# An expert stage written as a pipeline over pairs of experts: w2 of a pair between the experts of the next, small products grouped, weights in whole blocks

## The chip, the cores and the metric

The kernel runs on one core of a Trainium2 chip. The metric is the device time of one execution in microseconds (us), the median of several runs. The engines are TensorE (PE), VectorE (DVE), ScalarE (ACT), GpSimd (POOL) and SyncE (SP), which here issues nearly all transfers. PE's weight loads have a row of their own, PEld.

## The reference

Two layers of a hybrid block (a delta rule, pooling and sparse attention) are followed by two layers of a second block. A layer of the second block is a mixing part, a layernorm, a mixture of experts and another layernorm. There are 256 tokens of 1024 channels, 16 experts in four groups, and each token goes to two experts of one group. An expert has w1 and w3, each 1024 x 512, and w2, 512 x 1024. The part that the change touches is this:

```python
for l in range(DEPTH):
    h = _mixing(x, w_in[l], ...)
    x = _layernorm(alpha * x + h, ln1_g[l], ln1_b[l])
    m = _hier_moe(x.reshape(bsz * seq, d), w_group[l], b_group[l], w_expert[l], b_expert[l],
                  w1[l], w3[l], w2[l]).reshape(bsz, seq, d)
    x = _layernorm(alpha * x + m, ln2_g[l], ln2_b[l])

def expert_block(args):
    xb, e = args
    h = jax.nn.silu(xb @ w1[e]) * (xb @ w3[e])
    return h @ w2[e]
```

The results of the two experts of a token are weighted by its gates and summed.

## The kernel before

All weights stream from HBM once. Everything is in float32 or in float32 split into a high and a low part, and a float32 product of 512 columns leaves two records in the trace.

The expert stage gives each expert 64 slots. A token that finds no slot is handled by `overflow`, a dense computation over all experts behind a branch on the largest count (L1679 and L1690), which these inputs do not enter. The stage goes through the experts in groups of four, and within a group in pairs:

- **Gathers.** A product of the tokens (two blocks of 128, high and low part, zsh and zsl) with a one-hot matrix D picks the tokens of the four experts' 256 slots, one chunk of 128 channels at a time: four products for each of eight chunks. ACT or DVE (`affine`, L481 and L487) turns a chunk into xg. The gather of chunk k + 1 stands between the products of chunks k and k + 1 of the group's first expert.
- **w1 and w3** of an expert: the 64 slots of xg are the stationary operand, so a product takes half of the array's columns. w1 goes to the first half (j = 0), w3 to the second (j = 1), by turns, over eight chunks. ACT copies the result to `a` (L1604).
- **silu** (L1541): four transposes of `a` on PE, then ACT and DVE make hTe, the transposed hidden values. That of a pair's first expert stands within the second expert's products (at k = SILU_K), together with the transposed one-hot gT and the slots' gates; that of the second behind them.
- **w2** of the pair: for each half hf of the 1024 output columns, the four f-chunks of the first expert on one half of the array's columns and then the four of the second on the other. ACT and DVE evict a half, times the gate, into a high and a low part, yh (L1622) and yl (L1623).
- **add**: four products a half (two blocks of tokens, yh and yl) bring the slots' results back to their tokens, into sums in PSUM (pacc). One half of the pair before is added behind each of the pair's experts.

The branch stands between expert 7 and expert 8. In the second layer `rows` (L1658 to L1668) follows it: it spreads the gain and the bias of the last layernorm over all partitions by 32 products with diagonal matrices. All products of the helper `mm` carry the line L341; groups are told apart by their operands.

The weights of a layer are 192 blocks of 128 x 2 x 512 (0.5 MB), in the order of use: 24 for each pair, eight for w1 and w3 of each expert and eight for w2. `stream` (L1385 to L1405) issues them on SP into slots that it takes in turn; a slot comes free when PE has used the block in it, and SP waits for that in its queue. Some slots hold half a block or a quarter, which makes two or four transfers of the block. Of a layer's blocks FIRST + len(SOON) = 41 are issued ahead of the stage, during the mixing; those in SOON go last of them. The products are written in the order above; the layer that records them moves some of them a few places.

## Time and profile before

| | |
|---|---|
| runs | 1613.25 us, median of 3 (1613.2 to 1615.9) |
| span of the profiled execution | 1613.4 us |
| PE, DVE, ACT, POOL busy | 1550.3, 823.6, 670.2, 106.0 us |
| expert stage of layer 0, first gather to last add | 864.47 to 1121.84 us |
| expert stage of layer 1, first gather to last add | 1335.83 to 1602.1 us |
| granted PE clock over the span | 0.9 and more in every fortieth |
| bytes moved | 344 MB, 214 GB/s on the mean |

The profile is one execution, 0.15 us over the median of the runs. Busy times are sums over the span; matmuls are pipelined, so the busy time of a group on PE counts records that overlap only once. Where a row shows idle time before an instruction, the name behind the arrow is what ended it. A window's clock of 1.00 is the upper level.

### The profile page before, as it was taken

To read this page: it belongs to the slowest core of one execution; us is meant where nothing else is said; L and a number is where in the kernel's file an instruction comes from. 1 tells how busy PE (TensorE), PEld (TensorE's weight loads), DVE (VectorE), ACT (ScalarE), POOL (GpSimd) and SP (SyncE) were. 2 spreads that over 40 slices of the span, in tenths; PEclk is the share of its full clock that TensorE was granted. 3 is DMA by queue.
4 is the path that set the end of the run, shared out by engine and by line. 5 is a ranking of instruction groups with operands and counts; after the bars stand their busy time and mean duration, and the time that the engine had idled before them with its cause. 6 is when DMAs were issued, how large, how long until landed. Compare 5 with 4: busy or idle time off the path is not lost. (4 is left out here: it accounts for less than half of the span.)

```text
span 1613.4 us, 25627 instructions
## 1 busy us (share of the span) xinstructions
PE 1550.3 (96%) x9825; PEld 1107.2 (69%) x9826; DVE 823.6 (51%) x1897; ACT 670.2 (42%) x1383; POOL 106.0 (7%) x102
## 2 busy tenths in 40 slices
PE   8899999998999999999999998998999999998996
PEld 7877999988779999877775343343877774444332
DVE  6778656768786567567554111113567544112112
ACT  6536545565365455465543111112665542111111
POOL 3410000114100000200001000001000001000000
PEclk9999999999999999999999999999999999999999
DMA  7412664555126645444678999992356687998970
GB/s 263 148 54 74 209 184 144 182 159 151 54 75 209 183 143 173 148 151 150 231 274 282 343 357 354 376 378 93 99 164 212 235 277 268 332 381 322 387 291 27
DMA packets 149331, 344.47 MB, mean 214 GB/s; under 512 B 12112, under 2 KB 16848, under 8 KB 149200
## 3 DMA queue, kind: packets, MB, share of 16 engines
q1 hardware_dynamic: 149200, 342.74, 63.6%
q8 instruction: 81, 1.33, 0.3%
q14 instruction: 50, 0.41, 0.1%
HBM read 341.64 MB, written 1.05 MB: 212 GB/s over the span
## 5 line engine op out<-in xcount | busy, mean ns | idle before, releaser
L376 DVE TENSOR_TENSOR lo<-w,hi 128x1024 fp32r<-128x1024 f32 (+3 forms) x235 | 289.0, 1230 | 156.9 <-ACT hi L375 154.9
L375 ACT CAST hi<-w 128x1024 fp32r<-128x1024 f32 (+2 forms) x258 | 268.0, 1040 | 226.7 <-PE pd L341 175.2
L341 PE MATMUL p<-w,xg 128*64 128x512 f32 (+1 forms) x1044 | 265.2, 596 | 1.5 <-ACT xg L487 0.8
L341 PE MATMUL pd<-hTh,hi 128*128 128x256 f32 x768 | 218.7, 285 | 0.0
L341 PE MATMUL pd<-hTl,hi 128*128 128x256 f32 x768 | 218.4, 284 | 0.0
L341 PE MATMUL pd<-hTh,lo 128*128 128x256 f32 x768 | 218.2, 284 | 0.0
L341 PEld LDWEIGHTS p<-w,xg 128*64 128x64 f32 x1044 | 75.0, 136 | 113.4 <-issue 93.2
L341 PE MATMUL p<-w,hTe 128*64 128x512 f32 x496 | 148.1, 599 | 0.0
L341 PEld LDWEIGHTS pd<-hTh,hi 128*128 128x128 f32 x768 | 147.2, 192 | 0.2
L341 PEld LDWEIGHTS pd<-hTl,hi 128*128 128x128 f32 x768 | 147.2, 192 | 0.1
L341 PEld LDWEIGHTS pd<-hTh,lo 128*128 128x128 f32 x768 | 147.2, 192 | 0.1
L1550 DVE SCALAR_TENSOR_TENSOR t<-t,p 128x256 f32<-128x256 f32 x32 | 13.5, 421 | 191.9 <-ACT t L1547 191.9
L341 PEld LDWEIGHTS p<-w,hTe 128*64 128x64 f32 x496 | 50.1, 136 | 79.5 <-issue 75.0
L341 PE MATMUL pd<-hi,xTh 128*128 128x512 f32 (+2 forms) x224 | 86.7, 387 | 0.0
L341 PE MATMUL pd<-hi,xTl 128*128 128x512 f32 (+2 forms) x224 | 85.8, 385 | 0.0
L341 PE MATMUL pd<-lo,xTh 128*128 128x512 f32 (+2 forms) x224 | 84.9, 379 | 0.0
L1623 DVE SCALAR_TENSOR_TENSOR yl<-p,gslot,yh 128x512 fp32r<-128x512 f32 x32 | 24.0, 750 | 112.6 <-ACT yh L1622 104.9
L1604 ACT COPY a<-p 128x512 f32<-128x512 f32 x32 | 18.8, 587 | 138.2 <-PE p L341 123.3
L1622 ACT ACTIVATE yh<-p,gslot 128x512 fp32r<-128x512 f32 x32 | 22.0, 687 | 126.9 <-PE p L341 116.9
L376 POOL TENSOR_TENSOR lo<-w,hi 128x1024 fp32r<-128x1024 f32 (+2 forms) x23 | 55.6, 2430 | 171.0 <-ACT hi L375 165.1
L341 PE MATMUL pd<-lo,hTh 128*128 128x512 f32 (+1 forms) x160 | 62.7, 392 | 0.5 <-POOL lo L376 0.5
L341 PE MATMUL pd<-hi,hTh 128*128 128x512 f32 (+1 forms) x160 | 63.0, 394 | 0.0
(539 smaller groups left out, 2905.6 us busy)
## 6 DMA issues: line engine op xcount, KB each, us to landing
w<-in_w SPq DMA_DIRECT2D x320, 512.0 KB, 7.3
w<-in_p SPq DMA_DIRECT2D x244, 512.0 KB, 3.7
w<-in_w SPq DMA_DIRECT2D x110, 256.0 KB, 5.4
w<-in_p SPq DMA_DIRECT2D x8, 420.0 KB, 3.5
w<-in_w SPq DMA_DIRECT2D x20, 128.0 KB, 5.4
x<-in_w SPq DMA_DIRECT2D x4, 512.0 KB, 4.0
w<-in_p SPq DMA_DIRECT2D x4, 498.0 KB, 5.1
x<-in_x SPq DMA_DIRECT2D x4, 256.0 KB, 4.1
```

The costliest lines, as they stand in the source:

```text
L341: self.last = self.nc.tensor.matmul(out, lhsT, rhs, start=start, stop=stop, skip_group_check=True)
L375: r = self.nc.scalar.copy(hi, a)
L376: (eng or self.nc.vector).tensor_tensor(lo, a, hi.bitcast(F32), op=OP.subtract)
L1550: V.scalar_tensor_tensor(t, t, 1.0, ps[:, :, 0:64], op0=OP.add, op1=OP.mult)
L1604: A_.copy(a, ps)
L1622: A_.activation(yh, ps, AF.Copy, scale=gs_)
L1623: V.scalar_tensor_tensor(yl, ps, gs_, yh.bitcast(F32), op0=OP.mult, op1=OP.subtract)
```

## The change

The host lays out the experts' weights anew, as `we`: twelve blocks of 128 x 1024 for each expert, of which eight hold a chunk of w1 beside the same chunk of w3 and four hold w2. A transfer of a whole block then reads one row of 4 KB for each partition, where it read two of 2 KB before. The order of the blocks follows the new order of use, and the last blocks issued ahead of the stage are now numbers 4 to 7.

The loop goes over pairs. Between the two experts of a pair stands w2 of the pair before (`out_of_slots`), in which the two experts alternate. Both silus of a pair, gT and the gates stand in one place (`between`), two chunks into the next pair's first expert; the eight products of a pair's add in another, three chunks into the next pair's second expert. Gathers go four chunks at a time, and those of the next group stand within the second expert of the group's last pair. `rows` and its products are gone: `row` loads the gain and the bias with a transfer that reads the same row for all partitions.

PE, layer 0, the second half of w2 of one pair; hTe_10438 and hTe_10470 are the hidden values of its two experts. Before:

```order
L341 MATMUL p_10497<-w_10498,hTe_10438 64x512
L341 MATMUL p_10497<-w_10500,hTe_10438 64x512
L341 MATMUL p_10497<-w_10502,hTe_10438 64x512
L341 MATMUL p_10497<-w_10504,hTe_10438 64x512
L341 MATMUL p_10497<-w_10510,hTe_10470 64x512
L341 MATMUL p_10497<-w_10512,hTe_10470 64x512
L341 MATMUL p_10497<-w_10514,hTe_10470 64x512
L341 MATMUL p_10497<-w_10516,hTe_10470 64x512
```

With the change, of a pair behind the branch, with hTe_10880 and hTe_10890:

```order
L349 MATMUL p_10951<-w_10952,hTe_10880 64x512
L349 MATMUL p_10951<-w_10956,hTe_10890 64x512
L349 MATMUL p_10951<-w_10954,hTe_10880 64x512
L349 MATMUL p_10951<-w_10958,hTe_10890 64x512
L349 MATMUL p_10951<-w_10964,hTe_10880 64x512
L349 MATMUL p_10951<-w_10968,hTe_10890 64x512
L349 MATMUL p_10951<-w_10966,hTe_10880 64x512
L349 MATMUL p_10951<-w_10970,hTe_10890 64x512
```

The two experts' products now take turns, where four of one stood ahead of four of the other.

PE, layer 0, the place where a pair's silu and w2 stand (fc,a are the silu's transposes, eDb those of gT and the gates). Before:

```order
L1595 MATMUL p<-bc,eDb 128x128
L341 LDWEIGHTS eDb
L341 MATMUL p<-eG_10073,eDb 128x6
L341 LDWEIGHTS eDb
L341 MATMUL p<-eG_10073,eDb 128x6
L341 MATMUL p<-w,xg 64x512 x6
L341 MATMUL pacc<-yh,gT 128x512
L341 MATMUL pacc<-yl,gT 128x512
L341 MATMUL pacc<-yh,gT 128x512
L341 MATMUL pacc<-yl,gT 128x512
L360 MATMUL p<-fc,a 128x128 x4
L341 MATMUL p<-w,hTe 64x512 x16
```

With the change:

```order
L368 MATMUL p<-fc,a 128x128 x8
L1580 LDWEIGHTS eDb
L1580 MATMUL p<-bc,eDb 128x128
L1580 LDWEIGHTS eDb
L1580 MATMUL p<-bc,eDb 128x128
L349 LDWEIGHTS eDb
L349 MATMUL p<-eG_10073,eDb 128x6
L349 LDWEIGHTS eDb
L349 MATMUL p<-eG_10073,eDb 128x6
L349 MATMUL p<-w,xg 64x512 x12
L349 MATMUL p<-w,hTe 64x512 x16
L349 MATMUL p<-w,xg 64x512 x6
```

The silus of both experts stand in one burst, and w2 of a pair stands directly between products of w1 and w3; before, the second silu had a place with an add, and w2 stood behind it.

PE, layer 0, gathers of a later group (the products with D; p_ are the PSUM banks, so four products fill one chunk). Before:

```order
L341 MATMUL p_10341<-D_10310,zsh_9916 128x256
L341 MATMUL p_10341<-D_10310,zsl_9917 128x256
L341 MATMUL p_10334<-w_10318,xg_10316 64x512
L341 MATMUL p_10334<-w_10320,xg_10316 64x512
L341 MATMUL p_10349<-D_10309,zsh_9914 128x256
L341 MATMUL p_10349<-D_10309,zsl_9915 128x256
L341 MATMUL p_10349<-D_10310,zsh_9916 128x256
L341 MATMUL p_10349<-D_10310,zsl_9917 128x256
```

With the change:

```order
L349 MATMUL p_10212<-w_9878,xg_9996 64x512 x2
L349 MATMUL p_10212<-w_9880,xg_9996 64x512 x2
L349 MATMUL p_10212<-w_9882,xg_9996 64x512 x2
L349 MATMUL p_10267<-D_10203,zsh_9914 128x256
L349 MATMUL p_10267<-D_10203,zsl_9915 128x256
L349 MATMUL p_10267<-D_10204,zsh_9916 128x256
L349 MATMUL p_10267<-D_10204,zsl_9917 128x256
```

Four gather products stood between every two products of w1 and w3; now sixteen (the four shown and twelve more) stand between runs of six.

The diff, without the comments that it removes and, where the loop is written anew, without its old lines, which stand above:

```diff
-FIRST, SOON = 37, [10, 11, 6, 7]
+FIRST, SOON = 37, [4, 5, 6, 7]
...
-    for n in ("x", "pool_w", "w_uq_2", "w_ukv_2", "w1_2", "w3_2", "w2_2"):
+    we = np.empty((DEPTH, NE, 12, 128, D), np.float32)
+    for i, n in enumerate(("w1_2", "w3_2")):
+        we[:, :, :8, :, i * 512:i * 512 + 512] = np.asarray(inputs[n]).reshape(DEPTH, NE, 8, 128, 512)
+    w = np.asarray(inputs["w2_2"]).reshape(DEPTH, NE, 2, 2, 128, 2, 512)
+    we[:, :, 8:] = w.transpose(0, 1, 5, 2, 4, 3, 6).reshape(DEPTH, NE, 4, 128, D)
+    a["we"] = we
+    a["ln2"] = np.ascontiguousarray(np.stack([inputs["ln2_g_2"][DEPTH - 1], inputs["ln2_b_2"][DEPTH - 1]]))
+    for n in ("x", "pool_w", "w_uq_2", "w_ukv_2"):
         a[n] = np.ascontiguousarray(inputs[n])
...
         blocks = []
+        first = lambda e: [(e, k) for k in range(8)]
+        second = lambda e: [(e + j, 8 + i) for hf in range(2) for i in (hf * 2, hf * 2 + 1) for j in range(2)]
         for e in range(0, NE, 2):
...
+            late = e + 2 == NE
+            blocks += first(e) + (second(e - 2) if e and not late else []) + first(e + 1)
+        blocks += second(NE - 4) + second(NE - 2)
+        slots = chain(SLOTS_W, SLOTS_1, cycle(SLOTS_W))
 
         def stream():
-            k, once = 0, len(SLOTS_1)
+            at_x = iter(range(2))
             for i in order:
                 done = 0
                 while done < 8:
-                    tag, n = SLOTS_1[k - N1] if N1 <= k < N1 + once else SLOTS_W[(k - once * (k > N1)) % N1]
-                    k += 1
+                    tag, n = next(slots)
                     if tag == "x":
-                        t = self.x[:, k % 2]
+                        t = self.x[:, next(at_x)]
                     elif tag == "ring":
                         t = self.ring.tile([128, 1024], F32, name="w", tag="w")
                     else:
                         t = self.wp.tile([128, n * 128], F32, name="w", tag=tag, bufs=self.bufs[tag])
...
+                    nc.sync.dma_start(t, I["we"][(l,) + blocks[i]][:, done * 128:(done + n) * 128])
+                    have[i] += [(done + j, t[:, j * 128:(j + min(n, 4)) * 128]) for j in range(0, n, 4)]
                     done += n
                 yield
...
-            Db = self.sm.tile([128, 2, 4, SLOTS], BF16, name="eDb", bufs=1)
+            Db = self.sm.tile([128, 2, 4, SLOTS], BF16, name="eDb", bufs=2)
...
+        def gather(ks, Ds, xg):
+            for k in ks:
+                if k % 2 == 0:
+                    both = bank()
+                ps = both[:, k % 2 * 256:k % 2 * 256 + 256]
+                for tb in range(2):
+                    self.mm(ps, zs[tb][0][:, tok(k)], Ds[tb], tb + k % 2 == 0, False)
+                    self.mm(ps, zs[tb][1][:, tok(k)], Ds[tb], False, tb == 1)
+            for k in ks:
+                self.affine(k, xg[k], both[:, k % 2 * 256:k % 2 * 256 + 256], pv["ln1_g"][:, k:k + 1], pv["ln1_b"][:, k:k + 1])
+        def into_slots(e, after):
+            sl = slice(e % 4 * SLOTS, (e % 4 + 1) * SLOTS)
+            ps = bank()
+            for k in range(8):
+                for j, part in enumerate(weights()):
+                    for o, w in part:
+                        self.mm(ps[j * 64:j * 64 + 64, o:o + w.shape[1]], xg[k][:, sl], w, k == 0, k == 7)
+                for f in after.get(k, ()):
+                    f()
+            a = w2("a")
+            A_.copy(a, ps)
+            mid.append(a)
+        def silu(a):
             ps = bank().rearrange("p (f n) -> p f n", f=4)
             for f in range(4):
                 self.tr(ps[:, f], a[:, tok(f)])
             t, h = w1("t", 4, 64), w1("hTe", 4, 64)
             r = A_.activation(t, ps[:, :, 0:64], AF.Tanh, scale=0.5)
-            if last:
-                self.preload(LOG_EXP, r)
             V.scalar_tensor_tensor(t, t, 1.0, ps[:, :, 0:64], op0=OP.add, op1=OP.mult)
             V.tensor_tensor(h, t, ps[:, :, 64:128], op=OP.mult)
-            return h
-        def add(e, hfs=(0, 1), behind=None):
-            gT, ys = todo_y
+            return h, r
+        def between(e, Db):
+            hs, r = zip(*[silu(mid.pop(0)) for _ in range(2)])
+            if e + 2 == NE:
+                self.preload(LOG_EXP, r[-1])
+            gt = bank()
+            gb = gt[:, 0:128].bitcast(BF16)
+            pair = lambda tb: Db[:, tb, e % 4:e % 4 + 2].rearrange("p a n -> p (a n)")
+            for tb in range(2):
+                self.nc.tensor.transpose(gb[:, tok(tb)], pair(tb), b["identb"])
+            for tb in range(2):
+                self.mm(gt[:, 128:134], pair(tb), G[:, tb, e:e + 2].rearrange("p a n -> p (a n)"), tb == 0, tb == 1)
+            gT = w1("gT", dt=F32R)
+            V.tensor_copy(gT, gb)
+            gs = self.s("gslot", 1)
+            for j, o in ((0, slice(0, 64)), (1, slice(64, 128))):
+                V.tensor_reduce(gs[o], gt[o, 128 + j * 3:131 + j * 3], axis=AX.X, op=OP.add)
+            pairs[e] = (hs, gT, gs, [])
+        def out_of_slots(e, hf):
+            hs, _, gs, ys = pairs[e]
+            ps = bank()
+            for f0 in (0, 2):
+                wc = [weights() for _ in range(2)]
+                for f in range(2):
+                    for j in range(2):
+                        for o, w in wc[j][f]:
+                            self.mm(ps[j * 64:j * 64 + 64, o:o + w.shape[1]], hs[j][:, f0 + f], w, f0 + f == 0, f0 + f == 3)
+            yh, yl = w2("yh", dt=F32R), w2("yl", dt=F32R)
+            A_.activation(yh, ps, AF.Copy, scale=gs)
+            V.scalar_tensor_tensor(yl, ps, gs, yh.bitcast(F32), op0=OP.mult, op1=OP.subtract)
+            ys.append((yh, yl))
+        def add(e, hfs=(0, 1), behind=True):
+            _, gT, _, ys = pairs[e]
+            behind = self.last if behind else None
             for hf in hfs:
                 yh, yl = ys[hf]
                 for tb in range(2):
...
+                    for i, y in enumerate((yh, yl)):
+                        self.mm(acc[tb][hf], gT[:, tok(tb)], y, False, i == 1 and e + 2 == NE)
+                        if behind is not None:
+                            self.after(self.last, behind)
+        mid, pairs = [], {}
+        xg = self.chunks("xg")
+        gather((0, 1), Ds, xg)
+        gather((2, 3), Ds, xg)
+        last_Db = Db
+        for e in range(0, NE, 2):
+            if e == 8:
                 self.overflow(l, cnt, G2, zs, pv, acc)
...
+            if e + 2 == NE and l + 1 == DEPTH:
+                rows = [self.row("ln2", i) for i in range(2)]
+            todo_a, todo_b = {}, {}
+            if e == 0:
+                todo_a = {0: [lambda: gather((4, 5), Ds, xg)], 2: [lambda: gather((6, 7), Ds, xg)]}
+            else:
+                todo_a = {1: [lambda: between(e - 2, last_Db)]}
+            into_slots(e, todo_a)
+            last_Db = Db
+            if e == 0:
+                G, G2 = gates()
+                x1_half(0)
+                todo_b = {5: [lambda: seeds(0), lambda: x1_half(1)]}
+            elif e == 2:
+                todo_b = {2: [lambda: seeds(1), lambda: add(0)]}
+            elif e + 2 < NE:
+                todo_b = {2: [lambda: add(e - 2)]}
+            if e and e + 2 < NE:
                 for hf in range(2):
...
+                    out_of_slots(e - 2, hf)
+            if e % 4 == 2 and e + 2 < NE:
+                next_Ds, next_Db, _ = one_hot(e + 2)
+                nxt = self.chunks("xg")
+                for at, k in ((3, 0), (3, 2), (6, 4), (6, 6)):
+                    todo_b.setdefault(at, []).append(lambda k=k: gather((k, k + 1), next_Ds, nxt))
+            into_slots(e + 1, todo_b)
+            if e % 4 == 2 and e + 2 < NE:
+                Ds, Db, xg = next_Ds, next_Db, nxt
+        e = NE - 2
+        out_of_slots(e - 2, 0)
+        between(e, Db)
+        out_of_slots(e - 2, 1)
+        out_of_slots(e, 0)
+        add(e - 2)
...
+    def row(self, name, i):
+        t = self._t("hi", 1024, "row", (), F32)
+        a = self.I[name]
+        self.nc.sync.dma_start(t, bass.AP(tensor=a.tensor, offset=a.offset + i * D, ap=[[0, 128], [1, D]]))
+        return t
...
-        x1 = self.chunks("x1")
+        x1 = [self._t(tag, 1024, "x1", (4, T), F32) for tag in ("hi", "lo")]
+        x1 = [x1[k // 4][:, k % 4] for k in range(8)]
```

## Rows read from the trace of the kernel before

**Rows 1.** Stages' windows: us, busy by engine (x instructions), granted clock, DMA share, GB/s

```profile
864.40:986.60 122.20, 121.56 (x554) 50.85 (x554) 27.18 (x77) 20.15 (x38) 2.56 (x6) 1.00 0.94 338
...
993.20:1121.90 128.70, 126.26 (x530) 50.77 (x531) 22.12 (x51) 20.62 (x35) 1.36 (x3) 0.98 0.81 293
1336.00:1459.00 123.00, 122.77 (x554) 51.33 (x553) 27.37 (x78) 20.14 (x38) 2.31 (x6) 0.99 0.94 335
...
1470.00:1603.00 133.00, 128.28 (x531) 49.84 (x530) 21.94 (x48) 20.14 (x35) 0.75 (x2) 1.00 0.69 252
```

**Rows 2.** Timeline of PE, layer 0, one pair: start us, us, operation, count

```profile
964.62 0.50 PE L341 MATMUL pacc<-yh,gT 128*128 128x512 f32 x1
...
965.74 4.51 PE L341 MATMUL p<-w,xg 128*64 128x512 f32 x20
970.18 0.66 PE L360 MATMUL p<-fc,a 128*128 128x128 f32 x4
...
970.91 2.80 PE L341 MATMUL p<-w,xg 128*64 128x512 f32 x12
973.64 0.50 PE L341 MATMUL pacc<-yh,gT 128*128 128x512 f32 x1
...
975.22 8.97 PE L341 MATMUL p<-w,hTe 128*64 128x512 f32 x32
984.12 0.50 PE L341 MATMUL pacc<-yh,gT 128*128 128x512 f32 x1
```

**Rows 3.** The same view, w2 of the pair before that one

```profile
948.85 7.68 PE L341 MATMUL p<-w,hTe 128*64 128x512 f32 x29
```

**Rows 4.** The same view, gathers of layer 0's first group

```profile
867.64 1.08 PE L341 MATMUL p<-w,xg 128*64 128x512 f32 x4
868.65 0.39 PE L341 MATMUL p<-D,zsh 128*128 128x256 f32 x1
...
868.99 0.29 PE L341 MATMUL p<-D,zsh 128*128 128x256 f32 x1
869.12 0.28 PE L341 MATMUL p<-D,zsl 128*128 128x256 f32 x1
869.32 1.08 PE L341 MATMUL p<-w,xg 128*64 128x512 f32 x4
```

**Rows 5.** Groups of PE by shape, 1336 to 1603: busy, mean ns, idle before and releasers

```profile
L341 PE MATMUL p<-w,xg 128*64 128x512 f32 x502 | 132.2, 605 | 1.0 <-DVE xg L481 0.6 <-ACT xg L487 0.4
...
L341 PE MATMUL p<-D,zsh 128*128 128x256 f32 x64 | 19.8, 335 | 1.4 <-DVE D L1477 0.8 <-ACT xg L487 0.7
...
L341 PE MATMUL pacc<-yh,gT 128*128 128x512 f32 x32 | 13.7, 444 | 1.7 <-ACT yh L1622 1.7
```

**Rows 6.** PE at the overflow branch: timeline of both layers, then two windows

```profile
993.21 0.55 PE L341 MATMUL p<-D,zsh 128*128 128x256 f32 x1 [6.67 <-PEq L1690]
...
1458.38 0.73 PE L341 MATMUL pacc<-yl,gT 128*128 128x512 f32 x2
...
1470.07 0.36 PE L341 MATMUL p<-D,zsh 128*128 128x256 f32 x1
...
924.90:928.00 3.10, 2.92 (x19) 1.77 (x18) 1.20 (x2) 1.23 (x2) 0.00 (x0) 1.00 0.76 268
993.20:998.20 5.00, 4.99 (x16) 2.99 (x16) 0.54 (x1) 0.56 (x1) 0.00 (x0) 0.51 0.98 360
```

**Rows 7.** Windows, as in rows 1: single transfers of 4 KB rows; a saturated stretch

```profile
100.00:140.00 40.00, 39.87 (x587) 33.04 (x586) 26.18 (x80) 19.17 (x63) 1.59 (x4) 1.00 0.17 53
...
1000.00:1080.00 80.00, 79.29 (x351) 32.06 (x352) 13.35 (x32) 11.89 (x22) 0.75 (x2) 1.00 1.03 374
```

**Rows 8.** Costliest groups on the page: evictions of the expert stage

```profile
L1623 DVE SCALAR_TENSOR_TENSOR yl<-p,gslot,yh 128x512 fp32r<-128x512 f32 x32 | 24.0, 750 | 112.6 <-ACT yh L1622 104.9
L1604 ACT COPY a<-p 128x512 f32<-128x512 f32 x32 | 18.8, 587 | 138.2 <-PE p L341 123.3
L1622 ACT ACTIVATE yh<-p,gslot 128x512 fp32r<-128x512 f32 x32 | 22.0, 687 | 126.9 <-PE p L341 116.9
```

More of the change, by code (lines that the diff above doesn't have):

```diff
@@ L2 @@
 from contextlib import ExitStack, contextmanager
+from itertools import chain, cycle
 import numpy as np
@@ L1396, in stream @@
                         t = self.wp.tile([128, n * 128], F32, name="w", tag=tag, bufs=self.bufs[tag])
-                    if n < 4:
-                        nc.sync.dma_start(t, blocks[i][:, done // 4, done % 4 * 128:(done % 4 + n) * 128])
-                        have[i].append((done, t))
-                    else:
-                        t = t.rearrange("p (k n) -> p k n", n=512)
-                        nc.sync.dma_start(t, blocks[i][:, done // 4:(done + n) // 4])
-                        have[i] += [(done + 4 * k_, t[:, k_]) for k_ in range(n // 4)]
+                    nc.sync.dma_start(t, I["we"][(l,) + blocks[i]][:, done * 128:(done + n) * 128])
+                    have[i] += [(done + j, t[:, j * 128:(j + min(n, 4)) * 128]) for j in range(0, n, 4)]
                     done += n
@@ L1532, in seeds @@
                     self.seed(acc[tb][hf][:, tok(k)], x1t[k // 2][:, k % 2, tok(tb)], k == 0)
-        def gather(k, Ds, xg):
-            ps = bank()[:, 0:256]
-            for tb in range(2):
-                self.mm(ps, zs[tb][0][:, tok(k)], Ds[tb], tb == 0, False)
-                self.mm(ps, zs[tb][1][:, tok(k)], Ds[tb], False, tb == 1)
-            self.affine(k, xg[k], ps, pv["ln1_g"][:, k:k + 1], pv["ln1_b"][:, k:k + 1])
-        def silu(a, last=False):
+        def gather(ks, Ds, xg):
[21 more added lines that the diff above has]
+        def silu(a):
             ps = bank().rearrange("p (f n) -> p f n", f=4)
@@ L1631, in moe @@
+        e = NE - 2
[4 more added lines that the diff above has]
+        add(e - 2)
+        out_of_slots(e, 1)
+        add(e, behind=False)
         if l + 1 < DEPTH:
@@ L1656, in moe @@
                 nc.sync.dma_start(out[:, tb, cut(hf)], zh[tb][:, cut(hf)])
-    def rows(self, cols):
-        V = self.nc.vector
-        row = self._t("hi", 1024, "row", (), F32)
-        for hf in range(2):
-            ps = self.bank()
-            for k in range(4):
-                d = self.w1("diag")[:, :128]
-                V.tensor_scalar(d, self.c["ident"], cols[:, hf * 4 + k:hf * 4 + k + 1], None, op0=OP.mult)
-                self.mm(ps[:, k * 128:(k + 1) * 128], self.c["ones"], d, k == 0, k == 3)
-            self.nc.scalar.copy(row[:, hf * 512:(hf + 1) * 512], ps)
-        return row
+    def row(self, name, i):
[3 more added lines that the diff above has]
+        return t
     def overflow(self, l, cnt, G2, zs, pv, sums):
@@ L1698, in overflow @@
                 for f in range(4):
[L1699 removed]
+                    for i in range(2):
                         for j in range(4):
[L1701 to L1702 removed]
+                            src = I["we"][l][bass.ds(e, 1), j * 2:j * 2 + 2, :, i * 512 + f * 128:i * 512 + (f + 1) * 128]
+                            nc.gpsimd.dma_start(scr[j], src.rearrange("a k p n -> p (a k) n"))
                         for k in range(8):
```

81 lines of the change are left out of this document (1 added, 80 removed).

## The prediction, made before the changed kernel was run

> **What bounds the kernel now.** I read the kernel by stages first, because the busy shares of the page average over stages with different limits. [Rows 1] cut the two expert stages into their halves before and after the overflow branch. In each half PE is busy for 96 to 99.8% of the time at a granted clock of 0.98 to 1.00, while DVE and ACT are busy for less than a quarter. So the expert stages, some 257 us in layer 0 and 266 us in layer 1 with the stretch between the halves, end when PE has worked through its queue, and what counts is how PE's time is spent. The timeline of one pair of experts [rows 2] shows that: a w1/w3 product fills one half of the array's columns, w1 on one half and w3 on the other, so the records run two at a time. The run of 20 records lasts 965.74 to 970.18 = 4.44 us and the run of 12 970.91 to 973.64 = 2.73 us; the difference gives 0.43 us for two records side by side, and 0.14 us is left at the end of each run. Three things are not this work: w2, which takes 975.22 to 984.12 = 8.90 us for 32 records where 16 x 0.43 + 0.14 = 7.02 us would do; the bursts of full-array products between the runs; and idle time.
>
> The change leaves the first block and the mixing alone. Its sum is made against the profiled execution's 1613.4 us, 0.15 us over the median of the runs.
>
> **w2 side by side.** Now a half of w2 is four f-chunks of one expert and then four of the other; afterwards the two experts alternate. In [rows 2] w2 costs 8.90 - 7.02 = 1.88 us more than side by side. [Rows 3] are a second look, a pair with nothing between w2 and the next expert: from 948.85 to the add at 964.62 that opens [rows 2] = 15.77 us for 64 records, against 32 x 0.43 + 0.14 = 13.90, so 1.87 us too. That the tail of w2 overlaps with the next expert therefore gives nothing back. There are 8 pairs in a layer: 16 x 1.87 = 29.9 us.
> The Trainium skill ("TensorE: Matmul & The Clock Gate", The mechanism) says that products start and end strictly in program order. By that, four products of one expert would hold up the four of the other, w2 would take 32 x 0.43 = 13.8 us, alternating would give 16 x 6.9 = 110 us and the time would be near 1480. The rows differ with it: w2 takes 8.90 us, so most of the second expert's products already run beside the first's; the sum goes by the rows, and that time gets no chance of its own.
>
> **Fewer bursts.** In [rows 4] a chunk's gather and its two w1/w3 products take 867.64 to 869.32 = 1.68 us: 2 x 0.43 for the four records side by side, 4 x 0.12 for the four gather products (868.99 to 869.12 is one, at 0.12 to 0.13), and 0.34 that is neither: the change of form, there and back. Each interruption costs that, whatever is in it. Counting in PE's order what stands between runs of 64-column products, and not counting what only the overflow branch would run: before 57 bursts in layer 0 and 61 in layer 1; afterwards 33 and 32. Gathers make most of it (eight chunks a group one by one, afterwards four in a burst); the silus of a pair share one burst and its eight adds another. 53 x 0.34 = 18.0 us. The products themselves are as many as before, so nothing else goes. The bursts are longer, and what then could be late is their input; that is the first rival.
>
> **The gathers' lead and the other waits.** [Rows 5] give the idle time of layer 1 by what ended it: 1.0 us ahead of runs for gathered chunks, 0.7 us ahead of gathers for the eviction of an earlier chunk, and 1.7 us ahead of adds, which is the wait for yh at the very end, twice. The gathers now run one expert ahead, so the first two go (the 0.8 us for D stays, it is the start of the stage); of the last one half stays, since the last half of w2 still ends in an eviction and an add. That is 1.0 + 0.7 + 0.85 = 2.55 us in layer 1, and of layer 0, which has the same 1.7 us at its end, I take 0.85: 3.4 us.
>
> **The rows of the last layernorm.** In layer 1 the 32 diagonal products stand behind the branch. Its last product ahead ends at 1458.38 + 0.73 = 1459.11 and the gathers start at 1470.07: 10.96 us. Both times are in [rows 6]. In layer 0, without them, PE is idle for 6.67 us. There the restart is slow: twelve gather products and a run of four records take the 5.00 us of 993.2 to 998.2, at a granted clock of 0.51, the lower of the two levels (1.2 of 2.4 GHz), against the 3.10 us of 924.9 to 928.0 for the same work at full clock. So the branch alone costs 6.67 + 1.90 = 8.57, and the diagonal products 10.96 - 8.57 = 2.4 us. They go; the slow restart stays in both layers. The two row loads that take their place stand on SP's queue ahead of the last 32 blocks of 192. They need buffers that the last gathers free. If they were late, the blocks behind them would be, and PE would feel it only after the blocks already on the chip. I cost them at nothing; without that cover it would be 2 x 0.5 MB at 374 GB/s [rows 7], 2.8 us.
>
> **Weights in whole blocks.** The bytes are the same, in rows of 4 KB instead of 2 KB. SP has 41 of a layer's 192 blocks in its queue before the stage; 151 are left, 151 x 0.524 MB = 79.2 MB. At the 374 GB/s of a saturated stretch [rows 7] that is 212 us, and at the 338 GB/s of layer 0's first half [rows 1] 234 us, where SP also waited for free slots. By my sum the stages last about 233 and 236 us, and the last blocks are needed only at the end, so the transfers stay hidden, with less to spare than before (257 and 266). The blocks 4 to 7 of the first expert now come late in the preload; they are used some 7 us into the stage, and I cost that at nothing, with two waits of 0.85 us as a bound.
>
> **The sum.** 29.9 + 18.0 + 3.4 + 2.4 = 53.7 us; 1613.4 - 53.7 = 1559.7. Layer 0 gives 15.0 + 24 x 0.34 + 0.85 = 24.0, layer 1 15.0 + 29 x 0.34 + 2.55 + 2.4 = 29.8. Going through PE's order product by product with the same prices, where two 64-column products side by side need neighbours on different halves, gives 50 us for the first two terms instead of 47.9, since some bursts also split w2 and leave single records; with it 1557.6. I take **1558 us**. The price of an interruption has most play: 0.28 to 0.40 makes 15 to 21 us. The forecast's own range is 1550 to 1566.
>
> **Rivals.**
> 1. *The pipeline waits for itself.* A pair's w2 has its hT from a burst one run earlier; the silus wait for the copy of the second expert, only two steps (4 records a step, 1.7 us) behind its last product; the adds wait for yh and yl, 2.6 us behind w2. ACT's copy has a mean of 0.59, yh 0.69, yl 0.75 us [rows 8], so the silus need about 0.9 and the adds about 1.8 us, which fits, but not by much, and the PSUM banks are four as before. A missed one costs what such a wait costs now, 0.85 us for yh [rows 5]. Two for each pair: 32 x 0.85 = 27 us, so 1585. Against it: the distances above.
> 2. *The blocks come slower in whole rows, and the transfers set the end.* The stretch with 4 KB rows [rows 7] shows 53 GB/s at a share of 0.17, so 312 GB/s: 151 blocks then take 254 us from the stage's start. Both stages would last about 255 us: 1613.4 - 2.4 - 11.3 = 1600. That rate comes from single transfers far apart, while the 2 KB rows are read at 374 in a backlog, which speaks against it. The Trainium skill ("DMA: Bandwidth & Descriptors", Why small descriptors are slow (HBM only)) speaks against it as well: it gives each packet a fixed cost on the internal bus, which longer rows spread over more bytes. No row here shows whole blocks in a backlog.
> 3. *The same, and PE's clock falls between blocks: slower than before.* At 312 GB/s a block takes 1.68 us while PE uses one in 233 / 192 = 1.21; the 41 ahead are used up after 41 / (1/1.21 - 1/1.68) = 177 us, with 46 blocks to go. That is 56 us of PE at full clock and 111 at the lower level, which [rows 6] show behind a gap of 6.67 us. At that level a stage lasts 177 + 111 = 288 us: 1613.4 + 30.6 + 21.7 = 1666. It turns slower than now where the mean clock of that part is below 56 / (262 - 177) = 0.66. Against it: PE waits of 0.5 us a block are shorter than the gap in [rows 6].
> 4. *w2 gains nothing*, because the alternating products, each from another tile, cannot start in pairs: 1558 + 30 = 1588. Against it: w1 and w3 alternate in the same way and do.
>
> **How the numbers follow.** The forecast (faster than 1566) 0.75; rival 1 or part of it, 1566 to 1590, 0.12; rival 4 0.03; rival 2 0.04; rival 3 0.03; something that cancels the gain and that I don't see, 0.03. The range takes the forecast and half of the part of rival 1: **1547 to 1574**, with 3 us below the forecast's own range for the play of the burst price. A measurement of this kernel tells 0.2% (3.2 us) from no change. All of the forecast and rivals 1, 2 and 4 are faster: 0.94; same 0.02; slower 0.04.
>
> **What would show it.** After the change w2 of a pair should be 7.0 us inside its run, 33 and 32 bursts a layer should be left, the expert stages should last about 234 and 236 us, and the gap at the branch should be near 6.7 us in both layers. Waits of over 0.5 us ahead of silus or adds in each pair show rival 1; a run of w1/w3 that is spread by waits for blocks late in the stage, at a DMA share near 1, rivals 2 and 3; a w2 of 8 us or more rival 4. The prediction is wrong if the time is outside 1547 to 1574, or inside it with w2 not at 7 us.

## The result, and the profile after the change

The changed kernel takes **1539.2 us** (median of 4 runs, 1538.2 to 1539.6) against 1614.6 (median of 4, 1613.2 to 1616.2) for the kernel before: a ratio of 0.9533, with the 95% interval [0.952, 0.9547]. The forecast was 1558 with a range of 1547 to 1574. The direction was right, the time lies below the range: the change brought 76.4 us between the profiled executions (1613.4 and 1537.0), where the working gave 55.8.

The windows of the two expert stages of the kernel after, each cut at the branch as in [rows 1] (us, busy time by engine with instructions, granted clock, DMA share, GB/s):

```profile
863.80:967.10 103.30, 103.23 (x534) 47.12 (x534) 25.41 (x72) 19.43 (x37) 2.61 (x6) 1.00 0.92 349
971.50:1090.60 119.10, 118.19 (x550) 46.87 (x551) 23.57 (x56) 20.56 (x35) 1.39 (x3) 0.98 0.94 367
1304.40:1409.30 104.90, 104.71 (x534) 48.46 (x534) 25.49 (x71) 19.44 (x37) 2.68 (x6) 0.98 0.92 347
1409.90:1526.20 116.30, 115.39 (x548) 49.45 (x548) 22.29 (x52) 18.92 (x34) 0.74 (x2) 1.00 0.95 372
```

PE still has no idle time to speak of, and every part became shorter. From the first gather to the last add, layer 0 went from 257.4 to 226.7 us (30.6 less, forecast 24.0) and layer 1 from 266.3 to 221.6 (44.7 less, forecast 29.8). The gap at the branch is 4.5 us in layer 0 (967.0 to 971.6) and 0.7 us in layer 1.

One pair in layer 0 of the kernel after, PE's timeline (start us, us, operation, count):

```profile
940.06 1.09 PE L368 MATMUL p<-fc,a 128*128 128x128 f32 x8
...
941.22 5.37 PE L349 MATMUL p<-w,xg 128*64 128x512 f32 x24
946.42 7.04 PE L349 MATMUL p<-w,hTe 128*64 128x512 f32 x32
953.29 2.75 PE L349 MATMUL p<-w,xg 128*64 128x512 f32 x12
955.97 0.50 PE L349 MATMUL pacc<-yh,gT 128*128 128x512 f32 x1
```

This answers to [rows 2]: both silus in one burst, then w2 between products of w1 and w3, with no idle time on either side. The 32 records of w2 take 946.42 to 953.29 = 6.87 us, and the whole run of 68 records takes 14.75.

The groups of PE by shape in layer 1 (1304.4 to 1526.2), which answer to [rows 5]:

```profile
L349 PE MATMUL p<-w,xg 128*64 128x512 f32 x494 | 115.1, 598 | 0.7 <-ACTq L1716 0.7
...
L349 PE MATMUL p<-D,zsh 128*128 128x256 f32 x64 | 17.8, 314 | 0.8 <-DVE D L1476 0.8
...
L349 PE MATMUL pacc<-yh,gT 128*128 128x512 f32 x32 | 13.3, 426 | 0.8 <-ACT yh L1601 0.8
```

The waits for xg are gone, of the wait for yh one is left, and what is new is the 0.7 us of the branch. I summed PE's timeline of both stages by kind:

| part of the two stages | forecast, us less | measured, us less |
|---|---|---|
| runs of 64-column products (w2, single records, run ends) | 39.4 | 49.6 |
| bursts and waits outside the branch | 14.0 | 13.3 |
| the branch with the rows of the last layernorm | 2.4 | 12.4 |
| together | 55.8 | 75.3 |

The first two lines of the forecast share the 53 bursts: 0.34 us each are 0.14 of run end and 0.20 of the burst. The third line holds the gaps at the branch and, in layer 1, the diagonal products. So bursts and waits came as forecast in their sum, and two terms were too small by some 10 us each. The experiments go after these two, and after the two costs that I had set to nothing.

### The profile page after: what moved, and what is told of

The parts are those of the page before. It is cut to its first block, busy times and chain, and to the rows that moved or that the text cites. A ratio compares the mean times of both kernels' runs of the same rounds, so it can differ in the third digit from the quotient of the medians.

```text
span 1537.0 us, 25530 instructions
## 1 busy us (share of the span) xinstructions
PE 1486.4 (97%) x9793; PEld 1090.2 (71%) x9794; DVE 818.5 (53%) x1881; ACT 666.9 (43%) x1379; POOL 106.2 (7%) x102
## 3 DMA queue, kind: packets, MB, share of 16 engines
q8 instruction: 81, 1.33, 0.4%
## 5 line engine op out<-in xcount | busy, mean ns | idle before, releaser
L383 ACT CAST hi<-w 128x1024 fp32r<-128x1024 f32 (+2 forms) x258 | 268.0, 1040 | 226.3 <-PE pd L349 181.3
L349 PE MATMUL p<-w,xg 128*64 128x512 f32 (+1 forms) x1028 | 234.6, 593 | 5.2 <-PEq L1716 4.5
L349 PE MATMUL p<-w,hTe 128*64 128x512 f32 x512 | 118.1, 594 | 0.0
L349 PEld LDWEIGHTS p<-w,hTe 128*64 128x64 f32 x512 | 39.1, 137 | 70.1 <-issue 62.5
```

What stands on the lines that cost most here:

```text
L349: self.last = self.nc.tensor.matmul(out, lhsT, rhs, start=start, stop=stop, skip_group_check=True)
L383: r = self.nc.scalar.copy(hi, a)
```

## The experiments

The expectations name theories by letters: A is on w2's turns, C and D on what the scheduler's placing of bursts costs, E on the place of the code at the branch, G on where the silus stand, I on the length of the rows. A letter not listed is the rival of the one beside it. Every ratio is to the kernel before, timed on the same chip (1614.2 to 1615.1 us).

**w2_apart: after, with w2's products as before.**

```diff
-            for f0 in (0, 2):
-                wc = [weights() for _ in range(2)]
-                for f in range(2):
-                    for j in range(2):
+            wc = [[weights() for _ in range(2)] for _ in range(2)]
+            for j in range(2):
+                for f in range(4):
```

> The changed kernel with one part undone: in w2 of a pair the four products of the first expert come ahead of the four of the second again. Theory A (the forecast's price, four slots of 0.43 us lost for each pair): 16 x 1.87 = 29.9 us slower than the changed kernel, less about 2 us because its order has fewer split pairs: 1567. Theory B (alternating is worth more than the forecast's price, and that is where the additional gain comes from): 40 us slower or more, 1579 and up.

1562.3 us, ratio 0.9669 [0.9653, 0.9685]: 23.2 us more than the changed kernel. The same place as above in its timeline:

```profile
951.64 7.63 PE L349 MATMUL p<-w,hTe 128*64 128x512 f32 x29
958.68 0.64 PE L349 MATMUL p<-w,xg 128*64 128x512 f32 x1
...
960.02 3.11 PE L349 MATMUL p<-w,xg 128*64 128x512 f32 x9
963.06 0.50 PE L349 MATMUL pacc<-yh,gT 128*128 128x512 f32 x1
```

w2 and the products behind it last 951.64 to 963.06 = 11.42 us, against 946.42 to 955.97 = 9.55 with turns: 1.87 us, the price of the forecast. Summed over a layer, such runs exceed pure pairs by 12.2 us, and by 0.5 to 0.7 with turns; seven pairs of a layer have an expert behind them, so the mean is some 1.7 us each. The total of 23.2 is less than the 27.9 us of theory A. But the order of w2_apart also has three runs with an odd number of products in each layer where the changed kernel's has seven, and two bursts fewer in each. At 0.43 and 0.34 us those are some 4.8 us in its favour, so by this estimate the turns are worth some 28 us, near the forecast's 29.9.

**w2_turns: before, with the turns alone.**

```diff
-                    for j in range(2):
-                        wc = weights() + weights()
-                        for f in range(4):
+                    wc = [weights() + weights() for j in range(2)]
+                    for f in range(4):
+                        for j in range(2):
```

> The kernel before with one part of the change alone: w2 of a pair with its two experts by turns, all else and its place as before. Theory A: 29.9 us faster than before, 1584. Theory B: 40 us faster or more, 1574 and below.

1603.9 us, ratio 0.9936 [0.992, 0.9953]: 10.9 us gained, not 29.9. The pair of [rows 2] in its timeline, all engines:

```profile
973.82 8.54 PE L341 MATMUL p<-w,hTe 128*64 128x512 f32 x32
```

```profile
974.79 0.42 DVE L1551 TENSOR_TENSOR hTe<-t,p 128x256 f32<-128x256 f32 x1
975.27 0.19 PEld L341 LDWEIGHTS p<-w,hTe 128*64 128x64 f32 x3 [0.41 <-DVE hTe L1551]
```

The second expert's hidden values are there at 975.21. PE began at 973.82 with the first expert alone (four records start before 975.27), and from 975.27 the second expert's 16 records set the end: 16 x 0.43 + 0.14 = 7.02 gives 982.29, and the next add starts at 982.28. So w2 of this pair gains 0.4 us instead of 1.9. Waits in the two stages also grew, by some 6 us. The turns pay in full only if both experts' values are there when w2 begins, so in this kernel they need the pipeline.

**silu_late: after, with the silus directly ahead of w2** (`between` is called right before `out_of_slots`, not two chunks into the next pair).

> The changed kernel with the silus of a pair directly ahead of its w2 instead of one expert earlier; w2 keeps its turns and its place between the experts of the next pair. Theory G (w2 by turns pays only where hT of both experts is ready, which the early silu gives; in the kernel before with turns alone, PE ran the first expert's products alone until the second's hT came, 1.46 us behind the first record): 1.0 to 1.5 us for each of 12 to 14 pairs, 1553 to 1558. Theory H (the turns alone give the gain): no change, 1537 to 1541.

1554.6 us, ratio 0.9628 [0.9612, 0.9644]: 15.4 us lost. Timeline of one pair:

```profile
925.52 7.39 PE L349 MATMUL p<-w,hTe 128*64 128x512 f32 x31 [0.85 <-ACT t L1565]
```

Four pairs of each layer wait 0.85 us so, for ACT's tanh, and a fifth waits 0.46 us for hTe: 7.7 us in both layers. The runs of 64-column products also became 6.9 us longer. Seen from the other side, the same result: the distance between silu and w2 belongs to the gain of the turns.

**written_order: before, with PE's order pinned to the order of the code.** Every PE instruction of the stage is made to follow the one issued before it.

```diff
-        self.last = self.nc.tensor.matmul(out, lhsT, rhs, start=start, stop=stop, skip_group_check=True)
+        self.last = self.link(self.nc.tensor.matmul(out, lhsT, rhs, start=start, stop=stop, skip_group_check=True))
...
+    def link(self, r):
+        if getattr(self, "chain", None) is not None:
+            if self.chain:
+                self.after(r, self.chain)
+            self.chain = r
+        return r
```

> The kernel before, with PE's products of the expert stage held in the order in which they are written, so that no burst of small products stands between a w1 product and its w3 partner; nothing else is changed. Theory C (single records: where a burst splits a pair, a product runs alone, 0.43 us each, and the end of the stage in three pieces costs 3.5 us more; this is what the forecast left out): 17 to 21 us faster than before, 1593 to 1597. Theory D (splits cost no more than the interruption itself, and only the number of bursts counts, here 10 fewer): 3 to 4 us faster, 1610.

1599.8 us, ratio 0.9905 [0.9889, 0.9922]: 15.0 us gained without any edit of the kernel's work. One place in layer 0, first in the kernel before, then pinned:

```profile
1034.47 1.07 PE L341 MATMUL p<-w,xg 128*64 128x512 f32 x2
1035.48 0.44 PE L360 MATMUL p<-fc,a 128*128 128x128 f32 x2
1035.84 1.93 PE L341 MATMUL p<-w,xg 128*64 128x512 f32 x6
1037.70 0.44 PE L360 MATMUL p<-fc,a 128*128 128x128 f32 x2
```

```profile
1034.98 4.51 PE L341 MATMUL p<-w,xg 128*64 128x512 f32 x20
1039.42 0.66 PE L367 MATMUL p<-fc,a 128*128 128x128 f32 x4
```

Two records that find no partner take 1.07 us in the kernel before, as long as four in pairs [rows 4]. The scheduler had put transposes and other bursts between a w1 product and its w3 product. Counted in the records of the traces, bursts are 52 in each layer when pinned, instead of 56 and 60. Those 12 at 0.34 are 4.1 us, and waits grew by 3.9 us, so some 15 us are records without a partner. A run with an odd number of products leaves one such product, 0.43 us each: 13 and 17 such runs became one in each layer, 12.0 us. The rest is the end of the stage, where w2 of the last pair stood in pieces between adds. In the changed kernel grouping does part of the same: it has 3 such runs ahead of the branch in each layer, as before, but 4 behind it where there were 10 and 14, so 16 fewer or 6.9 us.

**gather_single: after, with gathers chunk by chunk** (24 bursts more).

> The changed kernel with the next group's gathers chunk by chunk (eight bursts of four products) instead of four chunks at a time. PE's order then has 24 bursts more in both layers together, with the same products. Forecast's term (0.34 us for each interruption whatever is in it): 24 x 0.34 = 8.2 us slower than the changed kernel, 1547. Rival (an interruption costs nothing beyond its products): 1539.

1546.3 us, ratio 0.9578 [0.9562, 0.9594]: 7.1 us lost, 0.30 for each burst, inside the 0.28 to 0.40 of the forecast. The intervals of the two ratios leave some 0.2 to 0.4. The two stages of the profiled executions became 6.1 us longer, with a new wait of 0.65 us in each.

**rows_2k: after, with blocks in two rows of 2 KB for each partition.**

```diff
-    a["we"] = we
+    a["we"] = np.ascontiguousarray(we.reshape(DEPTH, NE, 12, 128, 2, 512).transpose(0, 1, 2, 4, 3, 5))
```

> The changed kernel with its weights in two rows of 2 KB a partition and block again, as before the change; order of use, slots and products stay. Theory I (the transfers are hidden, so the form of the blocks is worth nothing): 1537 to 1542, with 374 to 388 GB/s in the saturated stretches where the changed kernel shows 404. Theory J (part of the additional gain comes from faster blocks): 1545 or more, with waits for blocks on PE.

1545.4 us, ratio 0.9569 [0.9551, 0.9586]: 6.2 us lost. The same stretch of both kernels, rows_2k first, then the changed kernel:

```profile
1000.00:1090.00 90.00, 89.22 (x426) 35.36 (x422) 19.37 (x46) 16.19 (x28) 0.00 (x0) 1.00 1.02 373
```

```profile
1000.00:1090.00 90.00, 89.17 (x425) 35.55 (x424) 19.58 (x46) 16.65 (x29) 0.03 (x1) 1.00 0.91 356
```

With 2 KB rows the 16 DMA engines are full for the whole stretch; with 4 KB rows a share of 0.09 is free. From 1440 to 1500 us, where they are full in both kernels, they move 387 GB/s in 2 KB rows and 402 in 4 KB rows. Layer 0 keeps its length (226.9), in layer 1 PE waits for blocks (0.4 us at the longest) and the stage takes 227.5 us instead of 221.6. So the shorter stage needs the long rows. What they would give the kernel before, whose transfers were hidden, was not tried.

**row_loads: before, with the rows of the last layernorm by transfers.**

> The kernel before with the gain and the bias of the last layernorm loaded as rows by transfers, so without the 32 diagonal products behind the branch. Forecast's term: 2.4 us faster than before. Theory E (the wait at the branch is a fetch of instructions whose length hangs on where the code lies, not on what stands there): the idle time at the branch in layer 1 is then anything from 0.7 to 6.7 us, the time up to 9 us lower than before, and layer 0's idle time stays 6.7 us since its code lies as before.

1617.1 us, ratio 1.0011 [1.0002, 1.0021]: nothing gained. PE behind the branch of layer 1, then late in the stage; below it SP's own wait at the second row load (total, times, longest us):

```profile
1461.23 0.36 PE L342 MATMUL p<-D,zsh 128*128 128x256 f32 x1 [0.28 <-PEq L1684]
...
1467.00 0.37 PE L342 MATMUL p<-D,zsh 128*128 128x256 f32 x1 [5.05 <-issue]
```

```profile
1542.62 4.50 PE L342 MATMUL p<-w,xg 128*64 128x512 f32 x8 [4.08 <-DMA w<-in_w]
```

```profile
SPq L1662 <- PE p L342: 39.2, 1, 39.2
```

The transfer waits 39.2 us for a buffer that the last gathers free, with all later blocks behind it, and PE pays late in the stage. In the changed kernel the gathers are done an expert earlier and no such wait is there. The branch itself costs 0.28 us here, and then PE stands still for 5.05 us in a straight line of code, four products on. The trace names no semaphore for that wait. Up to the first w1 product behind the branch the run without the diagonal products is faster: 7.0 us from the last add (1460.95 to 1467.95) instead of 12.3 (1459.11 to 1471.45), with eight gathers in both. So the diagonal products cost 5.3 us there, not 2.4, and the late transfers take it back.

**shift32 and shift64: after, with 32 or 64 products more in each mixing**, long before the expert stages. Their work is elsewhere; at the branch they change only where the code lies. I take the page's instruction queue q8 (81 packets, 1.33 MB, so 16.4 KB each) to be PE's, which has 19,587 instructions on the page (products and weight loads). By these numbers 32 products with their weight loads are an estimated 4 KB; they stand once ahead of layer 0's stage and twice ahead of layer 1's. Each was run once.

> The changed kernel with 32 more warming products at the start of each mixing part, far ahead of the expert stage, so that PE's code lies 32 products further on at the first layer's branch and 64 at the second's. Theory E (the idle time at the branch is a fetch of instructions, and its length hangs on where the code lies against the pieces in which it is fetched): the idle times at the two branches change from 4.5 and 0.7 us, by over 1 us in one layer at least; nothing else in the expert stage changes. Theory F (it hangs on what stands around the branch): both stay within 0.3 us. The added products make the mixing up to 2 x 5.5 us longer, so the two idle times are read, not the total.

> The same with 64 more, so 64 products further on at the first layer's branch and 128 at the second's. If a warming product is two instructions of 64 bytes, the second layer's code then lies one whole fetched piece (16384 bytes in the trace) further on: theory E in its strict form has the second layer's idle time at 0.7 us again, and the first layer's equal to the second's of the run with 32 in what concerns the shift alone. Theory F: 4.5 and 0.7 us.

PE's waits at the branch (total, times, longest us), shift32 in layers 0 and 1, then shift64 in layer 1:

```profile
PE p L349 <- PEq L1716: 4.7, 1, 4.7
...
PE p L349 <- PEq L1716: 4.0, 1, 4.0
```

```profile
PE p L349 <- ACTq L1716: 0.7, 1, 0.7
```

In layer 1 the same branch costs 0.70 us as built, 4.02 us 8 KB further on, and 0.68 us 16 KB further on, one whole packet. The stage takes 221.6, 226.3 and 220.3 us. So the 0.70 us of layer 1 is where the changed kernel's code happens to lie. Layer 0's gap did not move: 4.54 us as built, 4.66 with 4 KB, 4.50 with 8 KB.

**before_4k, before_8k, before_12k: the kernel before, with 32, 64 or 96 narrow products (16 columns, read by nobody) at the start.** Each was run once.

> The kernel before with 32 narrow products more at its start, where PE waits for the first rows: all of PE's code lies 4 KB further on. Theory E (the branch's idle time is a matter of placement, in the kernel before too): the stalls of 6.67 us in layer 0 and of 0.43 + 4.92 us in layer 1 change by over 1 us in this or the next two runs, to a total of 2 us or less in at least one layer and run. Theory K (the kernel before pays 5 to 7 us at any placement, and the change really took it away): 6 to 7 us and 5 to 5.5 us in all three runs.

> The same with 64 narrow products, 8 KB further on. Theory E: stalls that differ from those of the runs with 0 and 4 KB by over 1 us in one layer; theory K: 6 to 7 us and 5 to 5.5 us.

> The same with 96 narrow products, 12 KB further on. If theory E holds, the placement that is best for a layer is near one of the four, and the kernel before at a lucky placement would be 5 to 8 us faster, so that as much of the change's gain is luck. Theory K: 6 to 7 us and 5 to 5.5 us.

They take 1617.2, 1608.4 and 1615.3 us. At the branch of layer 0 PE waits 6.7, 0.9 and 6.7 us (6.67 unshifted [rows 6]), in layer 1 6.3, 6.3 and 6.2 us. The waits of before_8k, layers 0 and 1:

```profile
PE p L341 <- PEq L1692: 0.9, 1, 0.9
...
PE p L341 <- PEq L1692: 6.3, 1, 6.3
```

So the 6.67 us that I read as the price of the branch was a price of place too: 8 KB of idle products ahead of the stage take 7.7 us from layer 0's stage.

The traces also tell what arrives in such a gap. Of the DMA packets in the changed kernel's gap in layer 0, 967.03 to 971.58, one is of q8 (packets, MB, share of the 16 engines); in the 0.70 us of layer 1, 1409.21 to 1409.91, none is:

```profile
q8 instruction: 1, 0.02, 1.5%
```

It is the same in all runs of this document. In each of the 25 waits of 1.9 us or more at the branch or soon behind it, one packet of q8 lands, 1.2 to 1.9 us before PE goes on; in the waits of 1.13 us or less there, none lands. So the long waits are waits for code, as far as a coincidence without exception can show it.

**no_branch: after, without the overflow computation and its branch.**

> The changed kernel without the overflow computation and its branch (these inputs don't enter it). Prices what is left of the branch: in layer 0 4.5 us of idle time and some 1.8 us of slow restart, in layer 1 0.7 us and some 0.8: 7 to 8 us faster than the changed kernel, 1531 to 1532. If the fetch of the code behind the branch stalls PE in a straight line too, the idle time comes back elsewhere and the gain is below 3 us.

1528.8 us, ratio 0.9467 [0.9453, 0.9482]: 10.4 us. Layer 0's stage is 7.5 us shorter, layer 1's 2.7. That is more than the 7 to 8 us expected, and it bounds what the branch still costs; where the other 2 to 3 us lie was not followed up.

**both: after, with adds and silus in one burst and PE's order pinned; both_shift and both_placed: the same with the code shifted.** `both` has 22 bursts a layer instead of 33 and 32.

```diff
-                todo_a = {1: [lambda: between(e - 2, last_Db)]}
+                todo_a = {1: ([lambda: add(e - 4)] if e not in (2, 8) else []) + [lambda: between(e - 2, last_Db)]}
```

> A version that goes on from the change: a pair's adds stand with the next pair's silus in one burst, and PE's products of the expert stage are held in the order in which they are written. 22 bursts a layer where the changed kernel has 33 and 32, and no burst between a w1 product and its w3 partner: 21 x 0.30 = 6.3 us for the bursts (at the price that gathers chunk by chunk showed), 3 to 4 us for single records and the three pieces at the end of the stage: 1529 to 1531. If yh or hT come late in the longer bursts, 0.85 us for each such place.

> The same with 96 narrow products more at the very start, where PE waits for the first rows, and two wide ones fewer: all code lies some 12 KB further on. Theory E: the idle times at the two branches change again; with 0, 4 and 8 KB layer 0 had 4.5 to 4.7 us, with 0 and 16 KB layer 1 had 0.7 and with 8 KB 4.0. If layer 0's goes and layer 1's stays, 4 to 6 us faster than the version without; if both stall, 4 to 6 us slower; the added products cost up to 1 us.

> The version with adds beside silus and in written order, placed so that the first layer's branch lies 14 KB further on and the second's 16 KB (114 narrow products at the start with two wide ones fewer, 16 more at the end of the first expert stage). Theory E: layer 1 idles 0.7 us at the branch as without a shift; layer 0, which had 4.5 to 4.7 us at 0, 4 and 8 KB and 2.9 us at 12, 0.7 to 2 us. Then 2.5 to 5 us faster than the version without placement, less up to 1.5 us for the added products: 1525 to 1528.

`both` takes 1528.8 us, ratio 0.9465 [0.9452, 0.9478], 10.4 us under the changed kernel. `both_shift` gains in layer 0 what it loses in layer 1 (1528.3, 0.9458 [0.9443, 0.9472]). `both_placed`, with 114 narrow products at the start (two of the wide ones taken out) and 16 more behind the first expert stage, is the fastest: **1524.8 us, 0.9449 [0.9433, 0.9465]**. The group of w1 and w3 in its trace:

```profile
L349 PE MATMUL p<-w,xg 128*64 128x512 f32 (+1 forms) x1028 | 228.2, 589 | 4.0 <-issue 2.3 <-DVEq L1729 1.0 <-ACTq L1729 0.7
```

At its two branches it waits 1.0 and 0.7 us, and 2.1 us more for code right behind the first.

## Why the prediction missed

**w2 side by side (29.9): right, with a condition.** w2 takes 6.87 us where 7.0 were forecast, and w2_apart gives some 1.7 us for each of 14 pairs back, 23.2 us as measured and some 28 by the estimate above. But w2_turns got only 10.9 us: the term belongs to the turns and the earlier silus together.

**Fewer bursts (18.0): the price and the count were nearly right, the term beside them failed.** 33 and 32 bursts are left, as counted, at 0.30 by gather_single; before, the trace has 56 and 60 where I counted 57 and 61. What failed is the last step of the sum, "some bursts also split w2 and leave single records", with 2 us. Records without a partner cost the kernel before some 15 us (written_order), and some 10.5 of these are gone after the change. 6.9 us are the 16 split pairs. I had read 0.34 us from a place where the burst stands between whole pairs [rows 4] and gave it to all bursts; the extra 0.43 us of each place that splits a pair was in the rows of PE's timeline behind the branch, and my working did not use them. The end of the stage is of the same kind. Its w2 stood in pieces of 16, 12 and 4 records between adds, in layer 0 of the kernel before:

```profile
1106.34 5.42 PE L341 MATMUL p<-w,hTe 128*64 128x512 f32 x16
...
1113.25 3.70 PE L341 MATMUL p<-w,hTe 128*64 128x512 f32 x12
...
1117.55 1.93 PE L341 MATMUL p<-w,hTe 128*64 128x512 f32 x4
```

Together that is 11.05 us against the 8.97 of a w2 in one run [rows 2], so 1.8 us more in each layer beyond two run ends.

**The gathers' lead and the other waits (3.4): they went, with more than forecast.** That the sum with the bursts fits is partly luck. Bursts and waits together gave 13.3 us against 14.0. The waits alone gave 5.3 where the working had 3.4, and the bursts 8.0 where it had 10.6.

**The rows and the branch (2.4): wrong by 10 us.** The step that failed is "the slow restart stays in both layers", with a gap near 6.7 us in each. The 2.4 us failed with it: the working took layer 0's gap and restart off layer 1's 10.96 us, but layer 1 of the kernel before has rows of its own, which show another gap:

```profile
1459.54 0.68 PE L341 MATMUL p<-diag,fc 128*128 128x128 f32 x4 [0.43 <-DVE diag L1666]
1465.14 5.17 PE L341 MATMUL p<-diag,fc 128*128 128x128 f32 x28 [4.92 <-issue]
```

PE waits 0.43 us at the branch and 4.92 us four products on, and the diagonal products fill the other 5.6 us; row_loads gives 5.3 us for them. After the change PE starts again behind the branch so, in layer 0 and in layer 1:

```profile
971.58 3.68 PE L349 MATMUL p<-w,xg 128*64 128x512 f32 x8 [4.54 <-PEq L1716]
```

```profile
1409.91 1.94 PE L349 MATMUL p<-w,xg 128*64 128x512 f32 x8 [0.70 <-ACTq L1716]
```

Behind a gap of 4.54 us eight records take 3.68 us at a granted clock of 0.50, the lower level; behind 0.70 us they take 1.94 at 1.00. The slow restart comes with a long gap, and in layer 1 both are gone. 6.67 to 4.54 and 10.96 to 0.70 make 12.4 us. Of these the diagonal products are 5.6, which the edit earned. The other 6.8 are shorter gaps, 2.1 in layer 0 and 4.7 in layer 1. The shifts show that place in the code moves the gap, in the changed kernel's layer 1 and in the kernel before. So the 4.7 us of layer 1 are luck: its code lies well there as built, and 8 KB further on the gap is back at 4.02. That the 2.1 us of layer 0 are place too is not shown. The Trainium skill ("Runtime: NRT & Kernel Launch", Instruction fetch mechanics) says that a taken branch whose target is outside the window of code on the engine waits for a fetch. The dependence on place and the packet of q8 in each long gap agree; the 5.05 us in row_loads, four products behind the branch, show such a wait also in straight code.

**Weights in whole blocks (0): right here, for a reason that I had not shown.** The transfers stayed hidden at a DMA share of 0.92 to 0.95. By rows_2k the old rows would have cost 6.2 us.

**The rivals.** The pipeline does not wait for itself: the only waits above 0.5 us in the stages are the branch, the start for D, and yh at the end. The blocks are not slow (402 GB/s where the engines are full, not 312), so the clock does not fall between them, and w2 gained what it should.

That the time fell out of the range is these two terms: each was some 10 us too small, and had either gained only what was forecast, the time would be near 1549, inside it. The runs of 64-column products gave 12 us beyond the w2 and burst terms; by the counts above 6.9 are split pairs and 3.6 the pieces at the end, and the last 1 to 2 us stay open. That the waits at the branch end with a code packet is read from where the packets land; no run holds a packet back by itself.

## What to carry to other kernels

Read the timeline for records that stand alone: on an array used in halves, a burst that splits a pair costs as much again as the interruption, and a scheduler may place it there though the code does not. Alternating two streams pays only when the inputs of both are ready at its start, so look at the producer first. Before you credit an edit with a change of the gap at a branch, shift the code by some kilobytes without changing the work, and see whether the gap moves. And do not carry a gap from one layer over to another: read it in the rows of each.

## What the runs showed of the hardware

- The gap at the same branch with the same work was 0.7, 4.0 and 0.7 us in layer 1 of the changed kernel, with the code shifted by 0, 8 and 16 KB (estimated), and 6.7, 6.7, 0.9 and 6.7 us in layer 0 of the kernel before, with 0, 4, 8 and 12 KB. In layer 0 of the changed kernel it was 4.5, 4.7 and 4.5 us with 0, 4 and 8 KB.
- In each wait of 1.9 us or more at or right behind the branch, in all traces of this case, one 16.4 KB packet of the instruction queue q8 landed, 1.2 to 1.9 us before PE went on.
- Two 64-column records alone between bursts took 1.07 us, as long as four that run in pairs (1.08 us).
- A stall of 5.05 us stood in straight code four products behind a branch, with no semaphore named (row_loads).
- Over the same 60 us, with all 16 DMA engines full, rows of 2 KB moved 387 GB/s and rows of 4 KB 402 GB/s.
- One load that waits for its buffer held all blocks behind it on SP's queue for 39.2 us, and PE saw it late in the stage as a wait of 4.08 us.
